# Cross-covariance attention: V and output in 2 KB runs with two heads side by side, 16 output matmuls of 64 rows per unit instead of 32 of 32

## The chip, the cores and the metric

One core of a Trainium2 chip runs the whole kernel. The metric is the device time of one execution in microseconds (us); the lower the better. The profile's span runs from the first to the last instruction and is 1.8 us shorter than that time.

## The reference, cut to what matters

```python
# Q, K, V: (8, 12, 512, 64) float32 = batch, heads, n, d
Q_norm = Q / (np.linalg.norm(Q, axis=-2, keepdims=True) + 1e-10)   # over n
K_norm = K / (np.linalg.norm(K, axis=-2, keepdims=True) + 1e-10)
attn = np.einsum('bhnd,bhne->bhde', Q_norm, K_norm)                # 64 x 64 a head
attn = softmax(attn)                                               # over the last axis
out = np.einsum('bhnd,bhde->bhne', V, attn)                        # 512 x 64 a head
```

Each head is small, and Q, K, V and the output are 12.6 MB each: 50.3 MB go through the DMA engines whatever the kernel does.

## The kernel before

It works in 24 units of four heads. A unit's Q is one DMA of 512 KB: 128 partitions, 16 rows of 64 floats (4 KB) in each, so that a head fills 32 partitions. A software pipeline spreads one unit over several steps of a loop. In step s the tensor engine (PE) forms the gram matrices of unit s, doubles the attention matrix of unit s-2, multiplies V of unit s-3 with it, and so on. All DMAs are issued by SP, in order.

```python
HU, NV, R, TP = 4, 32, 16, 8          # heads of a unit, partitions of a head, rows of a partition, R // 2
Qf, Kf, Vf, Of = (... "(u p f) -> u p f", p=128, f=R * D ...)      # 4 KB runs
STORE_LAG = 6                          # LOAD_AHEAD 3, V_AHEAD 0

def grams(u):                          # 64 matmuls of 32 rows
    for t in range(R):
        for h in range(HU):
            x = qkb[u][NV * h:NV * (h + 1), t, :]
            nc.tensor.matmul(gbuf[:, h, 0:2 * D], x, x, start=(t == 0), stop=(t == R - 1), tile_position=(NV * h, 0))

def vtrans(u):                         # 8 transposes, one copy on ACT (L140)
    ...
def outs(u):                           # 32 matmuls of 32 rows, two copies on ACT (L160)
    s = so[u] = sop.tile([128, TP, 2 * D], F32, name="so")
    a = abuf[u % len(abuf)]            # [128, HU, 2, D]: the attention matrix twice on a diagonal
    for i in range(2):
        po = ps_o.tile([128, TP // 2, 2 * D], F32, name="po")
        for k in range(TP // 2):
            for h in range(HU):
                rows = slice(NV * h, NV * (h + 1))
                nc.tensor.matmul(po[rows, k, :], vt[u][:, TP // 2 * i + k, rows],
                    a[:, h].rearrange("p a d -> p (a d)"), tile_position=(0, NV * h))
        nc.scalar.copy(s[:, TP // 2 * i:TP // 2 * (i + 1), :], po)
...
for s in range(U + 3):
    on(load_qk, s + LOAD_AHEAD); on(load_v, s + V_AHEAD); on(store, s - STORE_LAG)
    on(cast_v, s - 2); on(cast_q, s + 1); on(normalise, s - 2); on(scale_k, s - 1)
    on(grams, s); on(norms, s); on(cast_k, s + 1); on(doubled, s - 2); on(keep_kq, s)
    on(outs, s - 3); on(logits, s - 1); on(scale_q, s - 1); on(exps, s - 1); on(vtrans, s - 2)
```

## Time and profile before

| | before |
|---|---|
| time, median of 3 runs | 142.27 us (141.93 to 143.15) |
| span of the profiled run | 140.5 us |
| PE matmuls, as many weight loads | 2616 |
| instruction blocks fetched for PE (q8) | 20 of 16 KB |
| DMA packets of 4096 bytes | 12288, median 159 ns |
| last V landed, last V cast | 119.0, 131.1 us |

Two lines of the page: the clock granted to PE in tenths of full speed, slice by slice, and the chain of work that ended last, followed back from the end, as shares of the span.

```profile
PEclk9999999995555599595569869985555797896555
PE 40%; issue 17%; ACT 14%; DMA 12%; DVE 11%; SPq 2%; ACTq 0%; DVEq 0%
```

The chain runs through PE for 40% of the span, and for another 17% through "issue", time in which an engine waits for nothing that the profile shows. DMA is 12% of it, although the DMA engines are full for four fifths of the span.

### The profile page before, as it was taken

Reading aid. Unit: us, or ns where it says so; the run is one execution under the profiler, and the core shown is the slowest. Engines: PE = TensorE matmul, PEld = TensorE weight load, DVE = VectorE, ACT = ScalarE, POOL = GpSimd, SP = SyncE. Lnnn points to the kernel's source line nnn. Section 1 sums busy time; section 2 is a strip of 40 time slices with the busy share of each in tenths; the row PEclk is TensorE's granted clock in tenths of the full one; section 3 lists DMA queues with packets and bytes.
Section 4 is the critical chain, followed back from the end, with each engine's and each line's share of the span. In section 5 each row is a group of like instructions: output and inputs, shape, how many; then the busy total and the mean of one; then the engine's idle time right before and its main releaser. Section 6 shows DMA issues by size and latency. Waiting matters only on the chain.

```text
span 140.5 us, 6167 instructions
## 1 busy us (share of the span) xinstructions
PE 95.7 (68%) x2616; PEld 73.1 (52%) x2616; DVE 93.9 (67%) x360; ACT 99.2 (71%) x169; POOL 40.1 (29%) x35
## 2 busy tenths in 40 slices
PE   0326698748688984956798397484989929857630
PEld 0325576536566763745566275263768617635420
DVE  0368989868585797857488488875768777754200
ACT  3011669859586898849489579967669888889960
POOL 6024344404302422503325304421505530320000
PEclk9999999995555599595569869985555797896555
DMA  4999999999999999999999999999999998223333
GB/s 171 367 400 421 409 411 405 407 402 407 412 414 418 413 419 411 409 416 411 415 413 421 411 414 416 413 420 412 420 411 414 412 392 323 112 97 154 149 149 149
DMA packets 13850, 50.71 MB, mean 361 GB/s; under 512 B 1536, under 2 KB 1536, under 8 KB 13824
## 3 DMA queue, kind: packets, MB, share of 16 engines
q1 hardware_dynamic: 13824, 50.34, 89.1%
q8 instruction: 20, 0.33, 0.9%
q14 instruction: 6, 0.05, 0.1%
HBM read 37.75 MB, written 12.58 MB: 358 GB/s over the span
## 4 chain that ended last, share of the span: by engine, by line
PE 40%; issue 17%; ACT 14%; DMA 12%; DVE 11%; SPq 2%; ACTq 0%; DVEq 0%
PE gram L88 15%; DMA vf<-in_V_dram 12%; PE po L156 9%; PE vps L138 8%; PE lgdup L116 6%; ACT so L160 5%; ACT vb L81 4%; DVE scr L100 3%; PE lgdup L145 3%; DVE ab L132 2%; DVE esum L128 2%; ACT ex L124 2%; ACT vt L140 1%; ACT ab L146 1%; DVE qkb L74 1%
## 5 line engine op out<-in xcount | busy, mean ns | idle before, releaser
L105 POOL TENSOR_TENSOR rq<-nsq,mhalf 128x4 f32<-128x4 f32 x24 | 37.7, 1569 | 84.8 <-DVE nsq L100 84.8
L88 PE MATMUL gram<-qkb 32*128 32x128 bf16 x1536 | 39.1, 269 | 22.4 <-issue 13.0
L88 PEld LDWEIGHTS <-qkb 32*128 32x128 bf16 x1536 | 32.1, 120 | 27.7 <-issue 16.5
L100 DVE CUSTOM_DVE_ANT_0 scr<-gram,ident 128x128 f32<-128x128 f32 x96 | 22.2, 287 | 11.6 <-PE gram L88 11.3
L160 ACT COPY so<-po 128x512 f32<-128x512 f32 x48 | 26.1, 589 | 4.1 <-PE po L156 3.5
L156 PE MATMUL po<-ab,vt 128*32 128x128 bf16 x768 | 21.8, 268 | 7.9 <-issue 6.8
L81 ACT CAST vb<-vf 128x1024 bf16<-128x1024 f32 x24 | 25.2, 1049 | 1.2 <-DMA vf<-in_V_dram 1.2
L156 PEld LDWEIGHTS <-vt 128*32 128x32 bf16 x768 | 15.3, 118 | 20.0 <-ACT vt L140 9.1
L140 ACT COPY vt<-vps 128x1024 bf16<-128x1024 bf16 x24 | 24.1, 1004 | 0.8
L138 PE MATMUL vps<-identb,vb 128*128 128x128 bf16 x192 | 20.5, 269 | 0.9 <-issue 0.9
L74 DVE CAST qkb<-qf 128x1024 bf16<-128x1024 f32 x24 | 16.3, 677 | 6.6 <-DMA qf<-in_Q_dram 6.6
L93 ACT COPY kq<-gram 64x256 f32<-64x256 f32 x24 | 8.8, 368 | 16.6 <-DVE nsq L100 16.4
L120 DVE TENSOR_TENSOR sl<-lgdup,rq 64x256 f32<-64x256 f32 x24 | 9.9, 414 | 11.5 <-PE lgdup L116 6.2
L138 PEld LDWEIGHTS <-vb 128*128 128x128 bf16 x192 | 15.0, 122 | 4.4 <-issue 3.5
L77 DVE CAST qkb<-kf 128x1024 bf16<-128x1024 f32 x24 | 16.5, 689 | 0.5 <-DMA kf<-in_K_dram 0.5
L146 ACT CAST ab<-lgdup 64x256 bf16<-64x256 f32 x24 | 8.8, 368 | 10.6 <-PE lgdup L145 10.2
L116 PE MATMUL lgdup<-ident,kqs 64*64 64x64 f32 x96 | 12.9, 273 | 2.4 <-ACT ab L146 2.4
L128 DVE TENSOR_REDUCE esum<-ex 64x4 f32<-64x256 f32 x24 | 9.8, 408 | 4.7 <-ACT ex L124 4.6
L145 PE MATMUL lgdup<-ab,identb 64*64 64x256 bf16 x24 | 8.2, 344 | 6.4 <-DVE ab L132 6.2
L124 ACT ACTIVATE ex<-sl 64x256 f32<-64x256 f32 x24 | 10.0, 418 | 3.4 <-DVE sl L120 3.3
L116 PEld LDWEIGHTS lgdup<-ident,kqs 64*64 64x64 f32 x96 | 7.9, 135 | 6.5 <-ACT ab L146 3.8
L110 DVE TENSOR_TENSOR kqs<-kq,rq 64x256 f32<-64x256 f32 x24 | 10.1, 423 | 0.8
(14 smaller groups left out, 28.8 us busy)
## 6 DMA issues: line engine op xcount, KB each, us to landing
qf<-in_Q_dram SPq DMA_DIRECT2D x24, 512.0 KB, 9.9
kf<-in_K_dram SPq DMA_DIRECT2D x24, 512.0 KB, 10.0
vf<-in_V_dram SPq DMA_DIRECT2D x24, 512.0 KB, 10.1
out_dram<-so SPq DMA_DIRECT2D x24, 512.0 KB, 9.9
```

Of the source, the lines that this page charges most:

```text
L74: nc.vector.tensor_copy(qkb[u][:, :, 0:D], qf[u])
L77: nc.vector.tensor_copy(qkb[u][:, :, D:], kf[u])
L81: nc.scalar.copy(w.rearrange("p t d -> p (t d)"), vf[u])
L88: nc.tensor.matmul(gbuf[:, h, 0:2 * D], x, x, start=(t == 0), stop=(t == R - 1), tile_position=(NV * h, 0))
L100: nc.vector.tensor_tensor_reduce(out=scr, in0=gbuf[:, h, 0:2 * D], in1=ident, scale=1.0, scalar=1e-20, op0=ALU.mult, op1=ALU.add, accum_ou ...
L105: nc.gpsimd.tensor_tensor(out=r, in0=n2, in1=mhalf, op=ALU.pow)
L116: nc.tensor.transpose(lg[:, h, :], kqs[u][D:, h, :], ident[D:, D:])
L124: nc.scalar.activation(e, sl[u], AF.Exp)
L138: nc.tensor.transpose(ps[:, t, :], vb[u][:, t, :], identb)
L140: nc.scalar.copy(w, ps)
L156: nc.tensor.matmul(po[rows, k, :], vt[u][:, TP // 2 * i + k, rows], a[:, h].rearrange("p a d -> p (a d)"), tile_position=(0, NV * h),)
L160: nc.scalar.copy(s[:, TP // 2 * i:TP // 2 * (i + 1), :], po)
```

## The change

V and the output of a unit are laid out as two groups of two heads. A head then fills 64 partitions with 8 rows (2 KB) each, and one output matmul covers 64 rows. Q and K keep their 4 KB runs. The intent is half as many output matmuls, for shorter DMA runs on half of the traffic.

```diff
-TP = R // 2
+SV = 2
+MV = 64
+TP = 4
-    Qf, Kf, Vf, Of = (... "(u p f) -> u p f", p=128, f=R * D ... (Q, K, V, out))
+    Qf, Kf = (... "(u p f) -> u p f", p=128, f=R * D ... (Q, K))
+    Vf, Of = (... "(u s p f) -> u p s f", s=SV, p=128, f=TP * 2 * D ... (V, out))
 ...                          # tiles of V, vb, vps, vt, so: [128, SV, TP, 128] for [128, 8, 128]
-        for i in range(2):
-            po = ps_o.tile([128, TP // 2, 2 * D], F32, name="po")
-            for k in range(TP // 2):
-                for h in range(HU):
-                    rows = slice(NV * h, NV * (h + 1))
+        for g in range(SV):
+            po = ps_o.tile([128, TP, 2 * D], F32, name="po")
+            for t in range(TP):
+                for x in range(2):
+                    rows = slice(MV * x, MV * (x + 1))
                     nc.tensor.matmul(
-                        po[rows, k, :], vt[u][:, TP // 2 * i + k, rows],
-                        a[:, h].rearrange("p a d -> p (a d)"), tile_position=(0, NV * h),
+                        po[rows, t, :], vt[u][:, g, t, rows],
+                        a[:, 2 * g + x].rearrange("p a d -> p (a d)"), tile_position=(0, MV * x),
                     )
```

More of the change, by code (lines that the diff above doesn't have):

```diff
@@ L34 @@
     U = B * H // HU
-    Qf, Kf, Vf, Of = (x.rearrange("b h n d -> (b h n d)").rearrange("(u p f) -> u p f", p=128, f=R * D) for x in (Q, K, V, out))
+    Qf, Kf = (x.rearrange("b h n d -> (b h n d)").rearrange("(u p f) -> u p f", p=128, f=R * D) for x in (Q, K))
+    Vf, Of = (x.rearrange("b h n d -> (b h n d)").rearrange("(u s p f) -> u p s f", s=SV, p=128, f=TP * 2 * D) for x in (V, out))
     ctx.enter_context(tc.manual_schedule())
@@ L65, in load_v @@
     def load_v(u):
-        vf[u] = vp.tile([128, R * D], F32, name="vf")
+        vf[u] = vp.tile([128, SV, TP * 2 * D], F32, name="vf")
         nc.sync.dma_start(out=vf[u], in_=Vf[u])
     def store(u):
-        nc.sync.dma_start(out=Of[u], in_=so[u].rearrange("p t d -> p (t d)"))
+        nc.sync.dma_start(out=Of[u], in_=so[u].rearrange("p s t d -> p s (t d)"))
     def cast_q(u):
@@ L79, in cast_v @@
     def cast_v(u):
-        w = vb[u] = vbp.tile([128, TP, 2 * D], BF16, name="vb")
-        nc.scalar.copy(w.rearrange("p t d -> p (t d)"), vf[u])
+        w = vb[u] = vbp.tile([128, SV, TP, 2 * D], BF16, name="vb")
+        nc.scalar.copy(w.rearrange("p s t d -> p s (t d)"), vf[u])
     def grams(u):
@@ L134, in vtrans @@
     def vtrans(u):
-        ps = ps_v.tile([128, TP, 128], BF16, name="vps")
-        for t in range(TP):
-            nc.tensor.transpose(ps[:, t, :], vb[u][:, t, :], identb)
-        w = vt[u] = vtp.tile([128, TP, 128], BF16, name="vt")
+        ps = ps_v.tile([128, SV, TP, 128], BF16, name="vps")
+        for g in range(SV):
+            for t in range(TP):
+                nc.tensor.transpose(ps[:, g, t, :], vb[u][:, g, t, :], identb)
+        w = vt[u] = vtp.tile([128, SV, TP, 128], BF16, name="vt")
         nc.scalar.copy(w, ps)
@@ L148, in outs @@
     def outs(u):
-        s = so[u] = sop.tile([128, TP, 2 * D], F32, name="so")
+        s = so[u] = sop.tile([128, SV, TP, 2 * D], F32, name="so")
         a = abuf[u % len(abuf)]
-        for i in range(2):
-            po = ps_o.tile([128, TP // 2, 2 * D], F32, name="po")
-            for k in range(TP // 2):
-                for h in range(HU):
-                    rows = slice(NV * h, NV * (h + 1))
+        for g in range(SV):
+            po = ps_o.tile([128, TP, 2 * D], F32, name="po")
+            for t in range(TP):
+                for x in range(2):
+                    rows = slice(MV * x, MV * (x + 1))
                     nc.tensor.matmul(
-                        po[rows, k, :], vt[u][:, TP // 2 * i + k, rows],
-                        a[:, h].rearrange("p a d -> p (a d)"), tile_position=(0, NV * h),
+                        po[rows, t, :], vt[u][:, g, t, rows],
+                        a[:, 2 * g + x].rearrange("p a d -> p (a d)"), tile_position=(0, MV * x),
                     )
-            nc.scalar.copy(s[:, TP // 2 * i:TP // 2 * (i + 1), :], po)
+            nc.scalar.copy(s[:, g], po)
     gbuf = ps_g.tile([128, HU, 512], F32, name="gram")
```

## The prediction

> **What bounds the kernel now.** I read the page first: total busy times, then the slices.
>
> ```profile
> PE 95.7 (68%) x2616; PEld 73.1 (52%) x2616; DVE 93.9 (67%) x360; ACT 99.2 (71%) x169; POOL 40.1 (29%) x35
> DMA  4999999999999999999999999999999998223333
> GB/s 171 367 400 421 409 411 405 407 402 407 412 414 418 413 419 411 409 416 411 415 413 421 411 414 416 413 420 412 420 411 414 412 392 323 112 97 154 149 149 149
> q1 hardware_dynamic: 13824, 50.34, 89.1%
> q8 instruction: 20, 0.33, 0.9%
> ```
>
> No compute engine is over 71% busy. The DMA engines are full for 33 slices (to about 114 us) at some 412 GB/s, then nearly idle for 26 us. So the transfers are not what ends the kernel; something behind them is late. The view of the tile vf says how late:
>
> ```profile
> L67 SPq DMA_DIRECT2D vf<-in_V_dram x24: 327/328/1131, 4.5 to 109.3; - x24
> L81 ACT CAST vb<-vf x24: 1043/1048/1052, 15.7 to 131.1; 128x1024 bf16<-128x1024 f32 x24
> DMA to landing us min/median/max: 9.7/10.1/11.3
> ```
>
> The last V is issued at 109.3, lands at about 119 and is cast at 131.1: 12 us on the shelf. The last K lands at 109.9 and its gram starts at 121.2, 11 us later; for unit 2 that distance was 2 us, for unit 8 already 10. So compute falls behind while only loads run (units 0 to 5, three transfers per unit), and afterwards keeps the distance. What sets its pace is in the waits of PE and in the timeline of PE:
>
> ```profile
> PEld L88 <- issue: 16.5, 18, 2.7
> PE gram L88 <- issue: 13.0, 8, 2.6
> PE po L156 <- issue: 6.8, 6, 2.2
> ...
> 61.23 0.62 PE L88 MATMUL gram<-qkb 32*128 32x128 bf16 x31 [1.67 <-issue]
> 61.79 0.29 PE L145 MATMUL lgdup<-ab,identb 64*64 64x256 bf16 x1
> 62.01 0.63 PE L156 MATMUL po<-ab,vt 128*32 128x128 bf16 x32
> 62.59 0.56 PE L116 MATMUL lgdup<-ident,kqs 64*64 64x64 f32 x4
> 63.08 1.04 PE L138 MATMUL vps<-identb,vb 128*128 128x128 bf16 x8
> 64.05 1.57 PE L88 MATMUL gram<-qkb 32*128 32x128 bf16 x52
> 67.53 0.51 PE L88 MATMUL gram<-qkb 32*128 32x128 bf16 x12 [1.91 <-issue]
> ```
>
> PE stops for nearly 2 us in the middle of a gram, waiting for nothing that the profile shows. Count the matmuls between the two stops: 31+1+32+4+8+52 = 128, each with its weight load: 256 instructions. The q8 row has 20 instruction packets of 0.33/20 MB = 16 KB. In the trace's packet records (no view prints them) one of these starts just before each stop (58.71, 64.92), and PE goes on 2.3 to 2.6 us after its start. So the stops are PE waiting for its own instructions. While the DMA engines are full these packets start at 40.12, 46.32, 52.50, 58.71, 64.92, 71.09, 77.18, 83.22, 89.43, 95.48: every 6.2 us, whether PE stopped or not. I take this as the bound: 128 matmuls per 6.2 us. A unit has 64+32+1+4+8 = 109 matmuls, so 109/128 x 6.2 = 5.28 us per unit; steps 6 to 22 (gram start to gram start, 32.2 to 121.2) measured 89.0/17 = 5.24. DMA needs 5.1 to 5.16 per unit (qf issues 52.25 to 98.72: nine units). The two lie within 3% of each other, which is why the backlog of 10 to 12 us stays from unit 8 on.
>
> **What the Trainium skill says.** "Runtime: NRT & Kernel Launch", section "Instruction fetch mechanics": instructions are streamed in blocks of 16 KiB, 256 instructions, the next fetched while the current one executes, the cost "mostly hidden". The block size agrees with the trace (256 between stops, 16 KB packets); "mostly hidden" does not, with stops of 1.7 to 2.6 us. "DMA: Bandwidth & Descriptors", section "Queues, rings and completion order": an engine alternates between queues only at packet boundaries, packets of about 9 to 17 descriptors. That fits a fetch that waits behind full queues; no record here shows the arbitration itself. Same page, "Why small descriptors are slow": a fixed cost per packet of some 3 cycles. The trace agrees in kind: 4096-byte packets took 159 ns (median), 4-byte ones 9 ns. "TensorE: Matmul & The Clock Gate", section "The mechanism" (row/col tiling): tiles run concurrently, starts some 4 ns apart. The trace agrees: the four 32-row output matmuls start 2 to 4 ns apart, and each group of four comes 56 ns after the previous one at full clock and 107 ns at half clock.
>
> **The change, part by part.**
>
> Array time of the output matmuls: nothing. Before, 8 groups of four 32-row matmuls at 56 or 107 ns; after, 8 groups of two 64-row ones, streaming the same 128 columns. 32 took 0.63 us at full clock and 1.05 at half; 16 should take the same within 0.05.
>
> PE instructions: 16 matmuls and 16 weight loads fewer per unit, 24 x 32 = 768 in all, of 2616+2616 = 5232: exactly three blocks of 256. So 17 fetches instead of 20, and 93 matmuls per unit: 93/128 x 6.2 = 4.50 us per unit instead of 5.28.
>
> DMA: V and output go from 4096 to 2 x 2048 bytes. A line through 9 ns at 4 bytes and 159 at 4096 gives 84 ns at 2048, so 168 for 159. A V or output DMA has 8 such rows per engine: 8 x 9 = 72 ns more; the records overlap by 3% (DMA share 1.03 in every full window), so 0.07 us. Steady state has two such DMAs per unit: 5.1 + 0.14 = 5.25 us per unit. If a fetch waits for whole packets its period grows as well, by the mean 2.8%: 6.37 us, and PE's pace is 93/128 x 6.37 = 4.63. Up to the last V, 24 V and 17 output DMAs precede: 41 x 0.072 = 3.0 us, so it lands at 122.0 instead of 119.0, and the last K, with 34 before it, at 112.4 instead of 109.9.
>
> ACT (vb 1.05, vt 1.00, two so 0.59 each) and DVE keep their shapes and work. The order on every engine is the same.
>
> Now the two paces are swapped: PE 4.6 per unit, DMA 5.25. While only loads run, compute still falls behind, but by 4.63 - 3.9 per unit, some 4 us by unit 6 instead of 8 to 10; after that it catches up by 0.3 to 0.6 per unit and should be close to the loads by unit 18 or so. The pure fetch bound puts the last gram at about 111 (13.6 blocks of 6.37 from the block that began at 24), the last K puts it at 112.4 + 2 = 114 or later. The bounds do not combine perfectly: with the clock at half, steps without a fetch stop still took 4.1 to 4.6 us. I expect the last gram at 115 to 118 instead of 121.2, centre 116.5. From there to the end took 140.5 - 121.2 = 19.3 us; with fewer PE instructions some 18.5. That is a span of 135.0; adding the 1.8 us between the time (142.27) and the span (140.46) gives 136.8, rounded down a little to 136.5 because the tail's fetches become fewer too.
>
> **Rivals.** (1) Fetch gain fully spent, DMA binds from the middle on: then compute sticks to the loads, the last V is cast at 122 or 123 instead of 131, and from that cast to the end it took 9.3 us: span 132, time 134. The 12 us of slack speak for it; against it, cold steps at 4.5 us leave little room to catch up. (2) The stops overlap other waits, so a removed fetch saves only its mean share: steps with a stop took about 5.6 to 6.7 us, those without 3.5 to 4.6, and 4 of some 14 fetches were hidden, so about 1.5 us each; three fewer give 4.4 us, time 138. The constant 6.2 us spacing speaks against it. (3) 2 KB runs are dearer than the line says: at 95 ns instead of 84, 8 x 2 x 11 = 0.18 us more for each of 41 DMAs, 7 us, last V at 129, span 139, time 140 to 141: no gain. Nothing in the trace shows a 2 KB packet, so this is the main danger. (4) PE array work was the bound and halving the output matmuls helps directly: no, the group spacing says their array time stays.
>
> **Range and chances.** Rivals 1 and 2 make 134 and 138, the centre is 136.5. The clock flips between full and half in stretches of 3 to 17 us in a pattern that will fall elsewhere, and moves the end by 1 to 2 us. 80%: 133.2 to 139.8. Over 2% faster means below 139.4: 0.84. Within 2%: 0.13, mostly rival 3. Slower: 0.03.
>
> **What would show it.** Right: 17 instruction packets on q8, still 6.2 to 6.4 us apart while DMA is full; output matmul groups at 56/107 ns, PE busy on that line hardly shorter per unit; 2048-byte packets at about 84 ns; the idle end of the DMA row shorter than 26 us; the last V cast nearer to its landing. Wrong: fetches that come at another spacing or stops that no longer matter, 2 KB packets well over 90 ns, or a last V that waits as long as before with no gain.

## The result, and the profile after

The changed kernel takes 136.51 us (median of 4 runs, 135.93 to 137.17) against 142.4 of the kernel before in the same rounds (141.93 to 143.15): ratio 0.9583, 95% interval 0.9517 to 0.9649. A ratio, here and below, is the mean time of one kernel's fast runs over that of the other's of the same rounds, so it is not quite the ratio of the medians.

From the page of the changed kernel (profiled run, span 135.4 us), the lines that answer to those above: busy times, clock, DMA row, instruction packets, chain by engine.

```profile
PE 87.9 (65%) x2232; PEld 68.3 (50%) x2232; DVE 95.1 (70%) x360; ACT 97.6 (72%) x169; POOL 36.5 (27%) x35
PEclk9999999999998699955599599599599599595555
DMA  4999999999999999999999999999999999997344
q8 instruction: 17, 0.28, 0.8%
DMA 67%; ACT 10%; PE 7%; DVE 6%; issue 5%; SPq 1%; ACTq 0%
```

There are 384 matmuls and three instruction blocks fewer. The DMA row is full to 36 x 3.38 = 122 us, so the idle end has shrunk from 26 us to 13 or 14. The chain has changed hands: 67% DMA and 5% "issue", where it was 12% and 17%. The waits of PE in the changed kernel (who waits for whom: us in total, times, longest):

```profile
PE lgdup L119 <- ACT ab L150: 16.2, 18, 1.8
PE lgdup L149 <- DVE ab L135: 12.1, 12, 2.1
PE gram L91 <- DVE qkb L80: 9.6, 3, 6.2
PE gram L91 <- issue: 3.1, 3, 1.5
PE vps L142 <- issue: 0.3, 1, 0.3
```

The waits on "issue" were 13.0 (gram) and 6.8 (output); they are 3.1 and none. PE now waits for ACT and DVE instead, and ACT in turn for V. The cast of V on the page before and after, the tile vf after, and ACT's timeline in steps 11 and 12:

```profile
L81 ACT CAST vb<-vf 128x1024 bf16<-128x1024 f32 x24 | 25.2, 1049 | 1.2 <-DMA vf<-in_V_dram 1.2
L84 ACT CAST vb<-vf 128x1024 bf16<-128x1024 f32 x24 | 25.1, 1047 | 15.0 <-DMA vf<-in_V_dram 14.8
```

```profile
L70 SPq DMA_DIRECT2D vf<-in_V_dram x24: 368/379/1224, 4.5 to 110.6; - x24
L84 ACT CAST vb<-vf x24: 1042/1046/1051, 15.9 to 125.8; 128x1024 bf16<-128x1024 f32 x24
```

```profile
59.17 1.01 ACT L144 COPY vt<-vps 128x1024 bf16<-128x1024 bf16 x1
61.05 1.04 ACT L84 CAST vb<-vf 128x1024 bf16<-128x1024 f32 x1 [0.87 <-DMA vf<-in_V_dram]
62.12 0.37 ACT L150 CAST ab<-lgdup 64x256 bf16<-64x256 f32 x1
62.40 0.37 ACT L96 COPY kq<-gram 64x256 f32<-64x256 f32 x1
62.78 1.07 ACT L164 COPY so<-po 128x512 f32<-128x512 f32 x2
63.74 0.42 ACT L127 ACTIVATE ex<-sl 64x256 f32<-64x256 f32 x1
64.23 1.01 ACT L144 COPY vt<-vps 128x1024 bf16<-128x1024 bf16 x1
66.12 1.05 ACT L84 CAST vb<-vf 128x1024 bf16<-128x1024 f32 x1 [0.87 <-DMA vf<-in_V_dram]
```

The first two lines are the group on the two pages: ACT idles 14.8 us for V, where it was 1.2. In the timeline ACT is through with its step at 65.2, sits idle for 0.87 us, and starts the next step when V lands. The cast of V is the first thing in ACT's step, so everything behind it waits too. From unit 8 to unit 20 V is cast within 0.2 us of its landing: 50.69 and 50.77 for unit 8, 113.13 and 113.20 for unit 20. Those landings are 62.44/12 = 5.20 us apart, and that is now the pace.

The array time of the output matmuls did not change. One step's group from the timeline of PE, at full clock; in the prediction the group of before stands at 62.01 with 32 matmuls and 0.63 us:

```profile
70.78 0.64 PE L160 MATMUL po<-ab,vt 128*64 128x128 bf16 x16
```

| | before | after |
|---|---|---|
| time, median | 142.4 us | 136.51 us |
| fetches, mean spacing 27 to 109 us | 20, 6.14 us | 17, 6.54 us |
| V landings, units 8 to 20, per unit | 5.12 us | 5.20 us |
| packet of 2048 bytes, median | none | 84 ns |
| last K landed, last gram started | 109.9, 121.2 us | 111.8, 116.1 us |
| last V landed, cast | 119.0, 131.1 us | 120.9, 125.8 us |

(Spacings and landings are read from the packet and semaphore records of the traces.) From 27.8 to 84.4 us the fetches of the changed kernel are 6.29 us apart on average; after that, up to 8.8 us. I read this as PE no longer asking for blocks as fast as they could come.

### The profile page after: what moved, and what is told of

It is laid out like the page before. It is cut to its first block, busy times and chain, and to the rows that moved or that the text cites. A ratio compares the mean times of both kernels' runs of the same rounds, so it can differ in the third digit from the quotient of the medians.

```text
span 135.4 us, 5399 instructions
## 1 busy us (share of the span) xinstructions
PE 87.9 (65%) x2232; PEld 68.3 (50%) x2232; DVE 95.1 (70%) x360; ACT 97.6 (72%) x169; POOL 36.5 (27%) x35
## 4 chain that ended last, share of the span: by engine, by line
DMA 67%; ACT 10%; PE 7%; DVE 6%; issue 5%; SPq 1%; ACTq 0%
DMA vf<-in_V_dram 54%; DMA qf<-in_Q_dram 14%; ACT so L164 3%; DVE scr L103 3%; ACT vb L84 2%; PE gram L91 2%; PE vps L142 2%; ACT ex L127 1%; ACT vt L144 1%; PE po L160 1%; PE lgdup L119 1%; DVE esum L131 1%; DVE ab L135 1%; ACT kq L96 1%; ACT ab L150 1%
## 5 line engine op out<-in xcount | busy, mean ns | idle before, releaser
L108 POOL TENSOR_TENSOR rq<-nsq,mhalf 128x4 f32<-128x4 f32 x24 | 34.1, 1419 | 83.0 <-DVE nsq L103 83.0
L91 PE MATMUL gram<-qkb 32*128 32x128 bf16 x1536 | 36.1, 260 | 12.7 <-DVE qkb L80 9.6
L91 PEld LDWEIGHTS <-qkb 32*128 32x128 bf16 x1536 | 30.4, 116 | 16.6 <-DVE qkb L80 10.1
L84 ACT CAST vb<-vf 128x1024 bf16<-128x1024 f32 x24 | 25.1, 1047 | 15.0 <-DMA vf<-in_V_dram 14.8
L160 PEld LDWEIGHTS <-vt 128*64 128x64 bf16 x384 | 14.4, 130 | 17.3 <-ACT vt L144 15.0
L119 PE MATMUL lgdup<-ident,kqs 64*64 64x64 f32 x96 | 11.6, 252 | 16.3 <-ACT ab L150 16.2
L160 PE MATMUL po<-ab,vt 128*64 128x128 bf16 x384 | 19.0, 255 | 1.2 <-ACT vt L144 1.2
L123 DVE TENSOR_TENSOR sl<-lgdup,rq 64x256 f32<-64x256 f32 x24 | 9.9, 414 | 13.8 <-PE lgdup L119 13.3
L142 PE MATMUL vps<-identb,vb 128*128 128x128 bf16 x192 | 18.8, 254 | 0.3 <-issue 0.3
L119 PEld LDWEIGHTS lgdup<-ident,kqs 64*64 64x64 f32 x96 | 7.1, 122 | 20.6 <-ACT ab L150 20.1
L149 PE MATMUL lgdup<-ab,identb 64*64 64x256 bf16 x24 | 7.9, 330 | 12.2 <-DVE ab L135 12.1
L142 PEld LDWEIGHTS <-vb 128*128 128x128 bf16 x192 | 13.7, 114 | 3.4 <-issue 1.8
L135 DVE TENSOR_TENSOR ab<-ex,rinv 64x256 bf16<-64x256 f32 x24 | 10.0, 417 | 0.8
```

The costliest lines, as they stand in the source:

```text
L84: nc.scalar.copy(w.rearrange("p s t d -> p s (t d)"), vf[u])
L108: nc.gpsimd.tensor_tensor(out=r, in0=n2, in1=mhalf, op=ALU.pow)
L119: nc.tensor.transpose(lg[:, h, :], kqs[u][D:, h, :], ident[D:, D:])
L142: nc.tensor.transpose(ps[:, g, t, :], vb[u][:, g, t, :], identb)
L160: nc.tensor.matmul(po[rows, t, :], vt[u][:, g, t, rows], a[:, 2 * g + x].rearrange("p a d -> p (a d)"), tile_position=(0, MV * x),)
```

## The experiments

Theory A is that of the prediction: before, PE was paced by the arrival of its own instructions, 256 per 6.2 us while the DMA engines are full. The change takes 32 of some 218 instructions out of each unit, and DMA becomes the bound. Theory B: the tensor array's time for the output matmuls mattered. Theory C: the 2 KB layout itself brings the gain. All results are set against the kernel before on the same chip, 142.1 us in each set (medians 142.11, 142.11, 142.06).

**1. two_kb_32: the layout alone.** The changed kernel with 32-row matmuls again (correct results).

```diff
-                for x in range(2):
-                    rows = slice(MV * x, MV * (x + 1))
+                for i in range(4):
+                    rows = slice(32 * i, 32 * (i + 1))
...
-                        a[:, 2 * g + x]..., tile_position=(0, MV * x),
+                        a[:, 2 * g + i // 2]..., tile_position=(0, 32 * i),
```

> The changed kernel with its 2 KB runs, but the output matmuls cut back to 32 of 32 rows (correct results): 109 matmuls per unit again. Theory A (instruction fetch paced the kernel before, 128 matmuls per 6.2 us; the change won by dropping 16 of them): 20 fetch packets, 109/128 x 6.3 = 5.4 us per unit, the whole gain lost: 142 to 145 us, the waits of PE for 'issue' back at 10 us or more. Theory B (the tensor array's time for the output matmuls was the bound): also about 142.4, but with the output groups before taking longer than those of 64 rows. Theory C (the 2 KB layout itself moves V and output better, or lands them better): stays at 136.5.

Measured: 143.25 us (141.97 to 143.83), ratio 1.0076 (1.002 to 1.0133); 20 fetches, 6.16 us apart. Its waits of PE:

```profile
PE gram L91 <- issue: 13.7, 8, 3.1
PE po L160 <- issue: 9.0, 6, 2.2
```

The whole gain is gone and the stops are back. C falls. The fetch spacing is the same as before, so it does not stretch with the packets' mix as the prediction had assumed. B already falls here, too: from the first to the last start of a unit's output matmuls it took 411 ns at full clock in this kernel and 418 in the changed one (732 and 751 at half clock), so the array gained nothing by the change.

**2. four_kb_16: fewer instructions alone.** The kernel before with 16 matmuls of 64 rows; two heads share one matrix, so half of the rows are wrong.

```diff
-                for h in range(HU):
-                    rows = slice(NV * h, NV * (h + 1))
+                for x in range(2):
+                    rows = slice(64 * x, 64 * (x + 1))
...
-                        a[:, h]..., tile_position=(0, NV * h),
+                        a[:, 2 * x]..., tile_position=(0, 64 * x),
```

> The kernel before with its 4 KB runs, but 16 output matmuls of 64 rows that use the wrong head's matrix for half of the rows (results wrong on purpose): the fewer instructions without the 2 KB runs. Theory A: 17 fetches, PE no longer the bound, DMA at 5.1 instead of 5.25 us per unit is, so the last V lands some 2 to 3 us earlier than in the changed kernel: 133 to 135.5 us, against 136.5 with 2 KB. Theory B: 136.5, no difference to the changed kernel. Theory C: 142.4, as before.

Measured: 134.61 us (134.39 to 134.84), ratio 0.948 (0.9453 to 0.9507), in the range of A. The last V landed at 118.4, against 120.9 with 2 KB runs. So the fewer instructions bring some 7.5 us, and the 2 KB runs, which make them possible with right results, take back about 1.9 (136.51 - 134.61, from two sets of runs).

**3. pad_tiny: the instructions back, with two columns each.** Ahead of every output matmul of the changed kernel stands one of two columns with the same weights and the same place, overwritten by it (correct results).

```diff
+                for x in range(2):
+                    rows = slice(MV * x, MV * (x + 1))
+                    nc.tensor.matmul(po[rows, t, 0:2], vt[u][:, g, t, rows],
+                        a[:, 2 * g + x].rearrange("p a d -> p (a d)")[:, 0:2], tile_position=(0, MV * x))
                 for x in range(2):
```

> The changed kernel with one more matmul of two columns, with its weight load, ahead of each output matmul, overwritten by it (correct results): the 32 instructions per unit are back, nearly none of the array time (16 x 2 columns). Theory A: 20 fetches, 142 to 145 us. Theory B and C: 136.5 to 137.5 us.

Measured: 144.37 us (143.88 to 145.32), ratio 1.0176 (1.0125 to 1.0226); 20 fetches, 6.15 us apart. The tile po (ns: least, median, most) and the waits of PE:

```profile
L160 PE MATMUL po<-ab,vt x384: 163/167/214, 20.9 to 137.1; 128*64 128x2 bf16 x192
L166 PE MATMUL po<-ab,vt x384: 222/223/315, 21.0 to 137.1; 128*64 128x128 bf16 x192
```

```profile
PE gram L91 <- issue: 11.5, 8, 2.6
```

The pads are not free on PE: a unit's output group, pads included, takes 668 ns from first to last start at full clock and 1197 at half, against 418 and 751 without pads. So the time alone does not separate the number of instructions from the array's work in this run; the stops do. The 11.5 us of waits on "issue" are back in gram, a place that the padding does not touch, and the fetches are as far apart as before. With run 1, where the array time was the same, B falls: the number of instructions counts. The time is that of two_kb_32 plus about 1 us, which may be the pads' own time; nothing here separates it.

**4. all_2kb: does more of the same help?** Q and K in 2 KB runs as well, gram with 32 matmuls of 64 rows (correct results).

```diff
+    Qf, Kf, Vf, Of = (... "(u s p f) -> u p s f", s=SV, p=128, f=TP * 2 * D ...)
-        for t in range(R):
+        for t in range(R // SV):
             for h in range(HU):
-                x = qkb[u][NV * h:NV * (h + 1), t, :]
+                y = MV * (h % 2)
+                x = qkb[u][y:y + MV, R // SV * (h // 2) + t, :]
```

> The changed kernel with Q and K in 2 KB runs as well, and 32 gram matmuls of 64 rows instead of 64 of 32 (correct results): 61 matmuls per unit, 2762 PE rows in the program. Theory A with DMA as the new bound: 48 more DMAs of 0.07 us put the last V 3.4 us later, at about 124; no stops for instructions are left, so the tail shortens a little: 136 to 139.5 us. If PE's instructions were still the bound after the change: 131 us or less. If 2 KB runs cost nothing: 134 to 136.

Measured: 139.58 us (138.34 to 139.62), ratio 0.9802 (0.9749 to 0.9855), just above the range that A with DMA as the bound gave (by 0.08 us). Only 11 fetches are left, and the kernel is about 3 us slower than the changed one. V landed 5.30 us apart, the last at 123.3. Its waits show ACT on V and nothing of weight on "issue":

```profile
ACT vb L83 <- DMA vf<-in_V_dram: 17.6, 15, 2.6
```

With DMA as the bound, removing more instructions did not pay here, and the shorter runs of Q and K cost. That is why Q and K are better left at 4 KB.

**5. no_k: less DMA, first try (failed).** The kernel before without its K loads, K cast from Q's tile (results wrong).

```diff
-        nc.sync.dma_start(out=kf[u].rearrange("p t d -> p (t d)"), in_=Kf[u])
-        nc.vector.tensor_copy(qkb[u][:, :, D:], kf[u])
+        nc.vector.tensor_copy(qkb[u][:, :, D:], qf[u])
```

> The kernel before without its K loads (K is cast from Q's tile; results wrong on purpose): every compute instruction stays, the DMA moves 37.7 instead of 50.3 MB and is no longer full from the middle on. If the 6.2 us between instruction blocks come from the fetch waiting behind full DMA queues: fetches come closer together than 6 us once the loads wait for buffers, the stops of PE shrink, and the unit takes 4.4 to 4.9 us: 120 to 132 us. If the fetch takes 6.2 us by itself, whatever the DMA load: still 5.3 us per unit, 138 to 142.

Measured: four runs of 134.56, 143.05, 133.72 and 139.12 us, the second and fourth slow. The two fast ones, about 134, lie between both expectations. Fetches came at uneven distances of 3.5 to 7.4 us, and PE still stopped for 11.6 us in gram. The transfers ran in bursts, with the DMA engines busy 78.5% of the span; the run tells nothing clear.

**6. five_loads: the DMA load taken away.** The kernel before; from unit 5 on the tiles of unit u-5 are used again and nothing is loaded (results wrong). All compute instructions stay.

```diff
     def load_qk(u):
+        if u >= 5:
+            qf[u], kf[u] = qf[u - 5], kf[u - 5]
+            return
     def load_v(u):
+        if u >= 5:
+            vf[u] = vf[u - 5]
+            return
```

> The kernel before with loads for the first five units only; later units compute on those tiles again (results wrong on purpose). All instructions of PE, DVE and ACT stay, the DMA carries stores alone from about 25 us on. no_k was too noisy to tell, so this takes the load away altogether. If the 6.2 us between fetches are made by full DMA queues: fetches of under 5 us when PE asks for them, stops of PE mostly gone, about 4.4 us per unit: 116 to 126 us. If a fetch takes 6.2 us by itself: 136 to 142 us.

Measured: 127.07 us (126.72 to 127.81), ratio 0.8934 (0.8885 to 0.8983). All 20 blocks are still fetched, on average 4.98 us apart from 27 to 109 us, with the shortest distances there at 4.3. Page and waits of PE:

```profile
DMA  4999999324404421441343144124304422443143
q8 instruction: 20, 0.33, 1.1%
DVE 45%; ACT 25%; issue 13%; PE 7%; DMA 5%; SPq 1%; ACTq 0%
```

```profile
PE gram L94 <- issue: 1.3, 2, 0.7
PE lgdup L151 <- DVE ab L138: 20.8, 20, 2.2
```

The same 5232 PE instructions run with 1.3 us of stops in gram instead of 13.0. So the slow fetches come from the DMA traffic, not from the fetch by itself, and the stops are not a fixed cost of each instruction. The transfer of a block is not what gets longer: in the packet records it takes 1.05 us (median) in the kernel before and 1.03 here. (In the kernel before, at the stops between 27 and 116 us, PE goes on 1.3 to 1.6 us after the packet has ended.) So what the traffic lengthens lies outside the packet itself. The time is 1 us above the range that I gave: what is left is the chain through DVE and ACT, which I had put somewhat too low.

**7. split_32: is it the bytes in the queues?** two_kb_32 with V and output as two DMAs of 256 KB each.

```diff
-        nc.sync.dma_start(out=vf[u], in_=Vf[u])
+        for g in range(SV):
+            nc.sync.dma_start(out=vf[u][:, g], in_=Vf[u][:, g])
```

(The store likewise.)

> two_kb_32 (2 KB runs, 32 output matmuls) with each V and output transfer as two DMAs of 256 KB, the same packets. The program keeps eight DMAs in flight, so some 25 to 30% fewer bytes stand in the queues. If the time of a fetch grows with what stands in the queues: fetches 4.5 to 5.5 us apart, 137 to 140 us. If it depends only on the DMA engines being busy: 6.2 us apart, 142 to 144 us as two_kb_32.

Measured: 141.48 us (141.4 to 143.34), ratio 0.998 (0.9896 to 1.0065); fetches 6.05 us apart instead of 6.16. A unit's six DMAs now average 341 KB instead of 512, so eight of them hold a third less in flight (more than the expectation says); from issue to landing they take 6.3 to 7.5 us (medians on the page) instead of 10.2 to 10.5. Yet the fetch distance fell by only 2%, far from what a wait in proportion to the queue would give. The time lies between the two ranges, and its interval does not tell it from the kernel before; the fetch distance is what decides here. What fixes the distance at some 6.1 us while the DMA engines are full stays open.

**8. halves: a smaller queue by half-height transfers (failed as a lever).** The kernel before, each DMA as two of 64 partitions.

```diff
-        nc.sync.dma_start(out=vf[u], in_=Vf[u])
+        for y in (0, 64):
+            nc.sync.dma_start(out=vf[u][y:y + 64], in_=Vf[u][y:y + 64])
```

(Q, K and the store likewise.)

> The kernel before with every DMA as two, of 64 partitions and 256 KB each, still in 4 KB runs: half of the bytes in flight. If the fetch waits for what stands in the queues: 6.2 falls to 4 to 5 us, PE no longer waits for instructions, DMA at 5.1 us per unit becomes the bound, 132 to 137 us. If not: 141 to 143. If 64 partitions cost the DMA engines bandwidth: GB/s well under 410 and a time over 143.

Measured: 184.35 us (181.53 to 187.14), ratio of the fast runs 1.2779. The profiled run was a slow one; the two fast runs took 181.5 and 182.3 us. The page:

```profile
GB/s 140 228 227 227 227 229 229 229 233 237 238 242 253 311 278 340 316 266 316 322 292 330 297 266 318 295 297 345 305 261 309 284 309 333 348 396 347 274 205 114
```

Where only loads run it moves 228 GB/s in this slow run, instead of 400 and more: the third case of the expectation. DMAs of 256 KB alone do not explain it, since split_32 has them for V and output and still moved some 400 GB/s. It says nothing about the fetch, since the kernel is bound by DMA throughout.

**9 to 11. lag8, lag10, lag12: can the new bound be moved?** If V's landing sets the pace, stores that stand ahead of V in the one queue cost time. The changed kernel with later stores (correct results):

```diff
-    STORE_LAG = 6
+    STORE_LAG = 10               # 8, 10, 12
-    sop = ctx.enter_context(tc.tile_pool(name="sop", bufs=10))
+    sop = ctx.enter_context(tc.tile_pool(name="sop", bufs=14))   # STORE_LAG + 4
```

> The changed kernel with stores issued 8 instead of 6 steps after the unit's loads, and two more output buffers: two stores fewer stand ahead of the last V. If DMA order sets the end (last V at 120.9): last V 2.6 us earlier, 133.5 to 135.5 us. If PE sets it: no change, 136 to 137.

> The same with 10 steps: four stores fewer ahead of the last V, which could land at 115.6. Then PE with its 4.5 to 4.6 us per unit (the fetch bound puts the last gram at about 111) is near the bound again: 131.5 to 134 us. If PE already set the end: 136 to 137.

> The same with 12 steps: the DMA has little left to give, PE's pace and the tail set the end: 130.5 to 134 us, less than 1.5 us under lag10; if stores pile up behind the last loads and end the kernel instead, above lag10.

Measured: lag8 133.98 us (133.65 to 134.77), ratio 0.9444 (0.9406 to 0.9481); lag10 133.36 us (133.17 to 133.45), ratio 0.9388 (0.9361 to 0.9415); lag12 133.61 us (133.56 to 134.34), ratio 0.9422 (0.939 to 0.9454). The DMA row of lag10:

```profile
DMA  4999999999999999999999999999999999999980
```

The last V of lag10 landed at 115.6, as worked out, and ACT's wait for V fell from 14.8 to 5.5 us. Its interval lies below that of the change alone (0.9517 to 0.9649), so lag10 beats both kernels. With 12 steps PE's stops are back (12.1 us of gram waiting on "issue", against 6.8 in lag10 and 3.1 in the changed kernel) and ten stores and more pile up at the end; DMA is full to the last slices and there is little left to move.

## Why the prediction was right

The time came out at 136.5, as predicted, and the main step, that instruction fetch is the bound before and DMA after, was shown by runs 1, 2, 3 and 6 (before) and by runs 2, 4 and 9 to 11 (after). Point by point:

- **The bound before.** Right. Fetches 6.14 us apart before, and still 6.15 to 6.16 in the two kernels that got their instructions back; with the DMA load gone, the same program runs without the stops.
- **Array time of the output matmuls.** Right: nothing. In the records the 64-row matmuls come at a mean distance of 27.9 ns at full clock, the 32-row ones at 13.3: half as many at twice the distance.
- **Three blocks fewer.** Right: 17. Their mean distance lay in the forecast 6.2 to 6.4 us up to 84 us (6.29); later it was longer, which I put down to PE waiting for DMA.
- **PE's pace after.** The 4.63 us per unit was too slow: grams 3 to 8 of the changed kernel started 4.20 us apart (18.94 to 39.95), grams 3 to 11 (to 53.16) 4.28. The 2.8% stretch of the fetch did not happen (run 1), which leaves 4.50; why these units ran faster still is not worked out.
- **DMA's pace after.** The packet time was right, 84 ns at 2048 bytes. Its effect was over-sized: 5.20 us per unit instead of 5.25, and the last V 1.9 us later (119.0 to 120.9) instead of 3.0. The packet records overlap, and I had allowed 3% for that; from 24 to 114 us the DMA share was 1.04 in the changed kernel against 1.03 before, and 5.27/1.04 - 5.12/1.03 is 0.10 us per unit, near the measured 0.08. Why they overlap more is open.
- **When compute catches up.** Too late: I said unit 18, looking at K alone. V stands three units later in the queue and had less slack; it bound from unit 8 on. This is rival 1's mechanism, which I had valued at 134.
- **The end.** The last gram began at 116.1 (predicted centre 116.5), and from there it took 19.3 us (18.5). So rival 1 was too short at the tail: it let the last V be cast as it lands, but the last V that was waited for was that of unit 20, cast at 113.2. Those of units 21 to 23 landed 2.5 to 2.7 us apart, since no Q and K were left to load, while the steps that cast them came 4.0 to 4.4 us apart. From 113.2 three such steps and 9.5 us lead to 135.4. Errors in both directions (PE and DMA both faster than predicted, the tail slower) left the sum where it was; the match to a tenth is partly luck.
- **The clock.** PE's mean granted clock rose from 0.76 to 0.84. It does not carry the result: one run of the kernel before had 0.80 and took 143.09 us, one of four_kb_16 had 0.81 and took 134.82; and three runs of all_2kb with 0.78, 0.79 and 0.85 took 139.62, 139.59 and 139.57 (the fourth, with 0.81, took 138.34).

## What to carry to other kernels

A wait that names nothing, "issue" in the middle of a run of matmuls, is worth counting out: if the stops lie 256 instructions apart and an instruction packet starts just before each, the engine waits for its program. Then, as here with full DMA engines, the number of instructions is the cost more than what each of them does, and a saving lasts only until the next bound, here DMA. Look beforehand for the stream with the least slack in that bound (V, not K): it also says what to do next, here to let the stores go later.

## What the Trainium skill lacked or had wrong

- "Runtime: NRT & Kernel Launch", section "Instruction fetch mechanics", calls the cost of crossing a 16 KiB boundary mostly hidden. With the DMA engines full a block came every 6.14 us (20 blocks), PE stopped for up to 2.6 us at a time, and 768 PE instructions fewer were worth about 7.5 us of 142 (142.11 to 134.61). With 167 GB/s of mean traffic instead of 361 (five_loads, before) the stops were nearly gone. No page warns that a full DMA queue slows the instruction stream.
- "DMA: Bandwidth & Descriptors", section "Why small descriptors are slow", gives the overhead per packet in cycles only (about 3), with nothing measured at 2 KB against 4 KB. Here two packets of 2048 bytes took 168 ns and one of 4096 took 159: 9 ns more by the records, while the end to end cost was 1.9 us over 41 DMAs of 8 extra packets per engine, 6 ns each. Whether the two agree is not settled.
- The same page, "Rules for kernel authors", advises against two transfers to disjoint partition halves because they gain nothing. Here they cost a great deal: 181.5 and 182.3 us in the fast runs instead of 142.1, and 228 GB/s instead of 400 while only loads ran (in a slow run).
- No page explains the 6.1 us between blocks. With a third fewer bytes in flight it fell only from 6.16 to 6.05 us.
